# Seven-product chunks of the MLP up projection: pairs of chunks in quarters of 512 columns, in place of single chunks in quarters of 256

## The chip, the cores and the metric

The kernel runs on one core of a Trainium2 chip. The metric is the device time of one execution in microseconds (us). The numbers of the profile come from one profiled execution of the same program. The engines are named as the profile names them: PE (matmul), DVE (elementwise on vectors), ACT (activations and copies), POOL, and SP, which here only issues DMAs.

## The reference

A trunk of two layers on 256 tokens with a model width of 2048, in 32-bit floats. Each layer is a token mixer (forgetting attention in the first, dilated windows in the second) and an MLP with a hidden width of 8192:

```python
def sq_relu_mlp(h, w_up, w_down):
    a = jax.nn.relu(h @ w_up)
    return (a * a) @ w_down

def reference(x, ...):
    for i in range(DEPTH):                       # 2 layers
        h = rms_norm(x, mix_norm_g[i])
        mix = fox_attention(...) if i % 2 == 0 else dilated_attention(...)
        x = x + mix
        h = rms_norm(x, mlp_norm_g[i])
        x = x + sq_relu_mlp(h, mlp_w_up[i], mlp_w_down[i])
    return x
```

The change is in the MLPs alone.

## The kernel before

**Products.** The 256 tokens are two halves of 128. Weights are read in tiles of 256 rows x 512 columns (512 KB, a *raw* tile). Each is split into a high part `wh` (ACT casts) and a low part `wl` (DVE subtracts), and the activations are split alike, so one product of 32-bit numbers is three matmuls: high x high, high x low, low x high. A *plain step* uses one raw tile: 2 blocks of 128 rows x 2 token halves x 3 = 12 matmuls of 512 columns (`product_steps`). A plain product of one 512-column chunk takes 8 steps and gathers in one pair of PSUM banks, one bank for each token half.

**The MLP's order.** It goes in four blocks `b` of 2048 hidden columns. Each block has four up chunks `n` of 512 columns and then a down projection with four products. Relu and square follow each up chunk, and the result is turned (transposed) by DVE in blocks of 32 and by way of DRAM (`turn_up`), then split into `aTh` and `aTl`, which are the stationary operands of the down product.

**Seven products.** Ten of the sixteen up chunks of a layer (three in block 1, three in block 2, four in block 3) are computed by a scheme that needs seven block products where eight are usual. For each tile of 256 rows it sees four quarters of the weights (128 rows x 256 columns) and four of the activations (128 rows x 128 tokens). `token_sums` makes four sums of the activations' quarters once for each MLP; `sum_quarters` makes three sums of the weights' quarters for every raw tile on DVE (tile `quarters`). Such a *slice* takes two split tiles, first the quarters themselves (768 columns) and then the sums (1024 columns), and 7 x 3 = 21 matmuls of 256 columns into halves of four banks (`slice_steps`, table `SEVEN`). `halves_chain` recombines the seven sums. Slices are woven between the plain steps of the block before, at steps that are written out in the tables `BETWEEN`.

**Order and lookahead.** The program is written out by one recording order. Helper chains are generators that advance by one *tick*: one for every half of a plain step and for every part of a slice. Weights are split five tiles ahead of their use: `split` is called when a tile is used up and prepares the fifth after it. Raw tiles lie in a ring of five (`RAW_BUFS`); `next_load` asks for the next raw tile when the oldest has been split. All these loads, and the DMAs of `turn_up`, are issued by SP in that order, and each engine works through its instructions in that order.

**Banks.** `sums` takes banks from a pool of four, so two plain products in a row use different pairs. The slices use the other four banks. In blocks 0 to 2 the down products are evicted by `add_chain` (`late`): ACT scales two halves of each bank into tiles `y`, and POOL adds them to the residual by DMA. The down products of a block are grouped, two at a time (three in block 3), so that the first half of the hidden chunks is used first.

Of the kernel before, what the change touches and what calls it, by code (L numbers as in the profile page):

```python
# [17 lines left out]
P = 128  # L18
D = 2048
# [22 lines left out]
DOWN_PARTS = ((0, 8), (8, 16))  # L42
# [7 lines left out]
BETWEEN = (-6, -5, -4, -2, 0, 1, 2, 3, 7, 8, 9, 10, 11, 12, 13, 15, 18, 19, 21, 22, 23, 24, 25, 26)  # L50
FIRST_BETWEEN = (0, 1, 2, 3, 4, 5, 6, 8, 11, 12, 13, 14, 15, 16, 17, 18, 22, 23, 25, 26, 27, 28, 29, 30)


LAST_BETWEEN = (-10, -9, -8, -6, -5, -4, -3, -1, 3, 4, 5, 6, 7, 8, 9, 11, 14, 15, 16, 17, 18, 19, 20, 22, 25, 27, 28, 30, 31, 32, 33, 35)
# [51 lines left out]
def trunk(ctx: ExitStack, tc, x, fox_w_in, fox_b_f, fox_q_gain, fox_k_gain, fox_w_out, dil_w_in,  # L106
# [4 lines left out]

    def clear(steps):

        return steps + (jobs.now + steps + 1) % 2
# [24 lines left out]
    ps_acc = ctx.enter_context(tc.tile_pool(name="ps_acc", bufs=4, space=PSUM))  # L139
# [13 lines left out]
    spare = ps_acc.tile([P, NC], F32, tag="acc", name="spare")  # L153
# [101 lines left out]

    def add(w, rows, cols):

        for r in range(rows[0], rows[1], RAW_SUB * P):
            units.append((len(plan), "rows"))
            plan.append((w, r, cols))  # L260
            for at in woven["due"].get(woven["count"], ()):
                units.extend(((len(plan), "quarters"), (len(plan), "sums")))
                plan.append(at)
            woven["count"] += 1

# [16 lines left out]
    def in_halves():  # L282

        for b in range(1, 4):
            for i, at in enumerate((FIRST_BETWEEN, BETWEEN, LAST_BETWEEN)[b - 1]):
                yield 40 * b - 8 + at, b, i // 8, i % 8

    def add_mlp(l):
        woven["count"] = 0
        for at, b, n, pr in in_halves():  # L290
            woven["due"].setdefault(at, []).append((mlp_w_up[l], pr * RAW_SUB * P, [(b * D + n * NC, NC)]))
        for b in range(4):
            if b == 0:
                add_group(*((mlp_w_up[l], [(n * NC, NC)]) for n in range(2)))
            for n in ((2, 3), (3,), (3,), ())[b]:
                add(mlp_w_up[l], (0, D), [(b * D + n * NC, NC)])
            down = mlp_w_down[l][b * D:(b + 1) * D]
            together = 3 if b == 3 else 2
            add_group(*((down, [(n * NC, NC)]) for n in range(together)), parts=LAST_DOWN_PARTS if b == 3 else DOWN_PARTS)
# [27 lines left out]
    state = {"raw": 0, "split": 0}  # L327
    raws, splits = [], []

    def load():  # L330
# [3 lines left out]
        w, r, cols = plan[i]  # L334
        t = wpool.tile([P, RAW_SUB, NC], F32, tag="raw", name=f"raw{i}", bufs=RAW_BUFS)
        at = 0
        for c, width in cols:
            src = w[r:r + RAW_SUB * P, c:c + width].rearrange("(c p) n -> p c n", p=P)
            hold(t)
            for rows in [slice(k, k + 1) for k in range(RAW_SUB)] if i == 1 else [slice(0, RAW_SUB)]:  # L340
                nc.sync.dma_start(t[:, rows, at:at + width], src[:, rows])
            at += width
# [16 lines left out]
    def split_part(i, part):  # L359
        nonlocal summing  # L360
        n, of = units[i]
        raw, (hi, lo) = raws[n], splits[i]
        if of == "sums":
            raw = quarters.pop()
        if of == "quarters":
            flat_hi, flat_lo, flat = (x.rearrange("p k n -> p (k n)")[:, 0:3 * HC] for x in (hi, lo, raw))
            nc.scalar.copy(flat_hi, flat)  # L367
            for _ in summing or sum_quarters(n):
                pass
            summing = None  # L370
            nc.vector.tensor_sub(flat_lo, flat, flat_hi.bitcast(F32))  # L371
            return
        nc.scalar.copy(hi[:, part, :], raw[:, part, :])  # L373

        coming = i + 1 < len(units) and units[i + 1][1] == "quarters"
        if coming:
            summing = sum_quarters(units[i + 1][0])
            next(summing)
# [859 lines left out]
```

## Time and profile before

| | |
|---|---|
| time, median of 3 runs | 2097.87 us (2097.11 to 2098.36) |
| profiled execution | 2098.41 us |
| its span, first to last instruction | 2096.7 us |
| PE busy | 2089.2 us, 11515 matmuls |
| DVE busy | 1774.4 us |
| ACT busy | 1296.4 us |
| DMA | 518.28 MB, mean 247 GB/s |

In rows of groups stand line, engine, operation, output<-inputs, shape, count, then busy time in us and the mean of one in ns, then the idle time of the engine ahead of them and what ended it. In rows of the order of time stand start and duration in us. In rows of waits stand the total in us, how often, and the longest. In tables of stretches stand busy us and count of each engine, the granted PE clock, the DMA share and GB/s. In rows of DMA issues stands last the median time from issue to landing in us. `halves_n` are the banks of the slices, `acc` those of plain products, `hT_n` the split activations, `sums_n` their sums, `room_n` the work tile of `token_sums`.

### The profile page before, as it was taken

The page shows a single profiled execution, that of the slowest core. Times are in us where ns is not written, and L with a number is a line of the kernel's source. Part 1 is how long each engine was busy: PE and PEld are TensorE (multiplying, and loading weights), DVE is VectorE, ACT ScalarE, POOL GpSimd, SP SyncE. Part 2 cuts the span into 40 slices and gives each one's busy share as a digit, 9 for nine tenths or more (in the row PEclk, how much of TensorE's full clock was granted, in tenths as well). Part 3 has the DMA queues.
Part 4 walks back from the last instruction along what each step waited for, and adds up shares of the span by engine and source line. Part 5 has one row for each costly group of instructions (what it writes and reads, how often), then busy time and mean ns, then how long its engine had stood idle before and what let it go on. Part 6 is the DMA issues. An engine that isn't in the chain of part 4 may idle for free.

```text
span 2096.7 us, 32543 instructions
## 1 busy us (share of the span) xinstructions
PE 2089.2 (100%) x11515; PEld 1877.3 (90%) x11515; DVE 1774.4 (85%) x2613; ACT 1296.4 (62%) x1895; POOL 134.8 (6%) x142
## 2 busy tenths in 40 slices
PE   9999999999999999999999999999999999999999
PEld 7888888889999999998888888888899998999998
DVE  6888876889999999998768787767899989999974
ACT  6665654766666666664655665645666766666663
POOL 2000000000100100110010010000001101000100
PEclk9999999999999999999999999999999999999999
DMA  8888877887887977887877776867878878788884
GB/s 257 255 261 267 253 245 223 273 263 240 259 243 245 265 239 256 261 256 232 281 239 230 247 241 212 264 207 238 282 235 259 243 250 243 234 251 258 265 265 151
DMA packets 375010, 518.28 MB, mean 247 GB/s; under 512 B 43112, under 2 KB 176576, under 8 KB 374848
## 3 DMA queue, kind: packets, MB, share of 16 engines
q1 hardware_dynamic: 360608, 503.23, 75.7%
q0 software_dynamic: 13824, 12.59, 4.0%
q8 instruction: 90, 1.47, 0.3%
q14 instruction: 72, 0.59, 0.1%
q10 hardware_dynamic: 416, 0.39, 0.1%
HBM read 463.12 MB, written 40.39 MB: 240 GB/s over the span
## 4 chain that ended last, share of the span: by engine, by line
PE 95%; DVE 2%; DMA 1%; issue 1%; ACT 0%; SPq 0%; ACTq 0%; DVEq 0%
PE acc L434 25%; PE acc L435 25%; PE acc L436 25%; PE halves_n L1069 6%; PE halves_n L1068 6%; PE halves_n L1067 6%; DVE wl L379 1%; DMA raw<-in_mlp_w_up_dram 1%; ACT wh L373 0%; PE sc_d L746 0%; DMA x<-in_x_dram 0%; PE sc_f L746 0%; PE po_d L695 0%; PE sc_d L743 0%; PE acc L482 0%
## 5 line engine op out<-in xcount | busy, mean ns | idle before, releaser
L379 DVE TENSOR_TENSOR wl<-raw,wh 128x1024 fp32r<-128x1024 f32 (+1 forms) x643 | 774.8, 1212 | 228.4 <-ACT wh L373 223.8
L373 ACT CAST wh<-raw 128x1024 fp32r<-128x1024 f32 (+1 forms) x643 | 663.8, 1043 | 393.7 <-PE acc L436 302.0
L434 PE MATMUL acc<-wh,hT_n 128*128 128x512 f32 x1280 | 486.4, 380 | 0.3 <-ACT hT_n L577 0.3
L435 PE MATMUL acc<-wl,hT_n 128*128 128x512 f32 x1280 | 485.4, 379 | 0.0
L436 PE MATMUL acc<-wh,hT_n 128*128 128x512 f32 x1280 | 485.3, 379 | 0.0
L373 ACT CAST wh<-quarters 128x1024 fp32r<-128x1024 f32 x160 | 167.9, 1049 | 265.9 <-DVE quarters L397 239.8
L436 PEld LDWEIGHTS acc<-wh,hT_n 128*128 128x128 f32 x1280 | 241.9, 189 | 34.6 <-DVE hT_n L578 0.4
L434 PEld LDWEIGHTS acc<-wh,hT_n 128*128 128x128 f32 x1280 | 242.2, 189 | 32.8 <-ACT hT_n L577 0.6
L435 PEld LDWEIGHTS acc<-wl,hT_n 128*128 128x128 f32 x1280 | 242.2, 189 | 32.6 <-DVE wl L379 0.5
L379 DVE TENSOR_TENSOR wl<-quarters,wh 128x1024 fp32r<-128x1024 f32 x160 | 194.9, 1218 | 40.9 <-ACT wh L373 40.9
L434 PE MATMUL acc<-wh,aTh_n1a 128*128 128x512 f32 x512 | 194.3, 379 | 0.0
L435 PE MATMUL acc<-wl,aTh_n1a 128*128 128x512 f32 x512 | 194.2, 379 | 0.0
L436 PE MATMUL acc<-wh,aTl_n1a 128*128 128x512 f32 x512 | 194.1, 379 | 0.0
L435 PE MATMUL acc<-wl,aTh_n3a 128*128 128x512 f32 x480 | 182.4, 380 | 0.0
L434 PE MATMUL acc<-wh,aTh_n3a 128*128 128x512 f32 x480 | 182.1, 379 | 0.0
L436 PE MATMUL acc<-wh,aTl_n3a 128*128 128x512 f32 x480 | 181.9, 379 | 0.0
L1067 PE MATMUL halves_n<-wh,sums_n 128*128 128x256 f32 x640 | 176.2, 275 | 0.0
L1069 PE MATMUL halves_n<-wh,sums_n 128*128 128x256 f32 x640 | 176.0, 275 | 0.0
L1068 PE MATMUL halves_n<-wl,sums_n 128*128 128x256 f32 x640 | 176.0, 275 | 0.0
L371 DVE TENSOR_TENSOR wl<-raw,wh 128x768 fp32r<-128x768 f32 x160 | 152.0, 950 | 0.0
L367 ACT CAST wh<-raw 128x768 fp32r<-128x768 f32 x160 | 133.1, 832 | 26.5 <-PE acc L436 12.0
L942 POOL DMA_DIRECT2D x<-y_n x96 | 84.2, 1357 | 970.3 <-ACT y_n L941 837.1
(655 smaller groups left out, 3527.3 us busy)
## 6 DMA issues: line engine op xcount, KB each, us to landing
raw<-in_mlp_w_up_dram SPq DMA_DIRECT2D x256, 512.0 KB, 5.1
raw<-in_mlp_w_down_dram SPq DMA_DIRECT2D x256, 512.0 KB, 4.8
raw<-in_dil_w_in_dram SPq DMA_DIRECT2D x192, 256.0 KB, 3.7
raw<-in_fox_w_in_dram SPq DMA_DIRECT2D x94, 512.0 KB, 4.8
raw<-in_fox_w_out_dram SPq DMA_DIRECT2D x32, 512.0 KB, 4.7
raw<-in_dil_w_in_dram SPq DMA_DIRECT2D x32, 512.0 KB, 4.9
raw<-in_dil_w_out_dram SPq DMA_DIRECT2D x32, 512.0 KB, 4.2
x<-y_n POOLq DMA_DIRECT2D x96, 128.0 KB, 5.9
```

What stands on the lines that cost most here:

```text
L367: nc.scalar.copy(flat_hi, flat)
L371: nc.vector.tensor_sub(flat_lo, flat, flat_hi.bitcast(F32))
L373: nc.scalar.copy(hi[:, part, :], raw[:, part, :])
L379: nc.vector.tensor_sub(lo[:, part, :], raw[:, part, :], hi[:, part, :].bitcast(F32))
L434: nc.tensor.matmul(acc[t], ah[:, tok], hi, start=first, stop=False)
L435: nc.tensor.matmul(acc[t], ah[:, tok], lo, start=False, stop=False)
L436: nc.tensor.matmul(acc[t], al[:, tok], hi, start=False, stop=last)
L942: nc.gpsimd.dma_start(xt[n][:, t, h * HC:h * HC + HC], y, accum_op=ALU.add)
L1067: nc.tensor.matmul(to, ah, hi, start=pr == 0 and not half, stop=False, skip_group_check=True)
L1068: nc.tensor.matmul(to, ah, lo, start=False, stop=False, skip_group_check=True)
L1069: nc.tensor.matmul(to, al, hi, start=False, stop=pr == KC // 2 - 1, skip_group_check=True)
```

## The change

The seven-product scheme now works on two neighbouring chunks, `n` and `n + 1`, at once. The quarters of the weights are 128 rows x 512 columns, one column half from each chunk, and each matmul has 512 columns. The number of chunks by seven products stays ten a layer: five pairs (`WIDE`). The other six chunks are plain (`UP_ALONE`).

Six of the seven products of a row block are done in three *slots* of two products, 6 matmuls each. A row block of a pair brings two raw tiles, each by two DMAs. The slots use three split tiles in turn: the quarters that lie crosswise (`crossed`), differences, and sums. DVE makes the differences from both raw tiles, and the sums out of them, in the tile `quarters`. The raw tiles are used up only when the sums are made. The seventh product (first quarter of the weights with first quarter of the activations) is done after all eight row blocks, in a *sweep*: four raw tiles hold the needed rows of the first chunk, read a second time, and their four slots add into bank 0 after ACT has copied the first product out of it.

The table of places is replaced by a rule (`wide_slots`): from step 17 of each MLP on, one slot follows each plain step, and two after the last step of each plain product; a pair's sweep and the next pair are set apart by at least one plain step.

The six sums of a pair take six whole banks: the four of before and one pair from the pool of plain products. So while pairs are under way every plain product of the MLP uses the same pair of banks (`turn["only"]`), and the evictions are recorded inside the product's last step and no longer after it. The down products of blocks 0 to 2 are no longer grouped. In `turn_up` the way through DRAM is held open until the place for the result is free, and the tiles are read back only then.

```diff
-DOWN_PARTS = ((0, 8), (8, 16))
-SEVEN = ((0, 0, 2, 5), (1, 0, 0, 4), (2, 0, 1, 0), (3, 0, 7, 6), (0, 1, 5, 3), (1, 1, 6, 2), (2, 1, 4, 1))
+PRODUCTS = (((0, 1, 5), (1, 0, 0)), ((2, 0, 1), (3, 1, 3)), ((4, 0, 2), (5, 1, 6)))
+WIDE = ((1, 0), (2, 0), (2, 2), (3, 0), (3, 2))
+WIDE_FROM = 17
+UP_ALONE = ((2, 3), (2, 3), (), ())
+def wide_slots():
+    todo = []
+    for b, n in WIDE:
+        todo += [(b, n, what, pr) for pr in range(KC // 2) for what in range(3)] + [None]
+        todo += [(b, n, 3, pr) for pr in range(0, KC // 2, 2)] + [None]
+    count = WIDE_FROM
+    while todo:
+        room = full = 2 if count % 8 == 7 else 1
...
-    ps_acc = ctx.enter_context(tc.tile_pool(name="ps_acc", bufs=4, space=PSUM))
+    ps_acc = ctx.enter_context(tc.tile_pool(name="ps_acc", bufs=2, space=PSUM))
...
+    def add_slot(w, c, what, pr):
...
+        if what == 0:
+            woven["at"] = len(plan)
+            for columns in ((NC, 0), (0, NC)):
+                plan.append([((k, slice(0, NC)), w[r + k * P:r + k * P + P, c + columns[k]:c + columns[k] + NC])
+                             for k in range(RAW_SUB)])
+        units.append((woven["at"], ("crossed", "differences", "sums")[what]))
...
+        if of == "crossed":
+            sums_of[0] = work.tile([P, RAW_SUB, NC], F32, tag="sd", name=f"quarters{n}", bufs=1)
+            nc.vector.tensor_sub(sums_of[0], raw, raws[n + 1][:, 1, :].unsqueeze(1).to_broadcast([P, RAW_SUB, NC]))
+        elif of != "rows":
+            raw = sums_of[0]
         nc.scalar.copy(hi[:, part, :], raw[:, part, :])
         nc.vector.tensor_sub(lo[:, part, :], raw[:, part, :], hi[:, part, :].bitcast(F32))
+        if of == "differences":
+            nc.vector.tensor_add(raw[:, 0, :], raws[n][:, 0, :], raw[:, 1, :])
+            nc.vector.tensor_sub(raw[:, 1, :], raws[n + 1][:, 0, :], raw[:, 0, :])
...
-        n = units[state["split"] - 1][0]
-        whole = state["split"] == len(units) or units[state["split"]][0] != n
-        if whole and state["raw"] == n + RAW_BUFS:
+        n, of = units[state["split"] - 1]
+        spent.update({"rows": (n,), "differences": (n, n + 1)}.get(of, ()))
+        while state["done"] in spent:
+            state["done"] += 1
+        while state["raw"] < min(len(plan), state["done"] + RAW_BUFS):
             load()
...
-    def sums(pool=ps_acc, tag="acc"):
+    def sums(pool=ps_acc, tag=None):
+        if tag is None:
+            tag = f"acc{turn['next'] if turn['only'] is None else turn['only']}"
+            turn["next"] = 1 - turn["next"]
...
+            if post is not None and k == KC - 1:
+                jobs.spawn(post(acc))
...
-                if t == 0:
-                    yield clear(1)
...
-    def slice_steps(tag, banks, pr):
+    def slot_steps(tag, banks, what, pr):
+        hi, lo = splits[used[0]]
+        for bank, i, a, of in [(0, i, 4, pr + i) for i in range(2)] if what == 3 else [(*x, pr) for x in PRODUCTS[what]]:
...
+            nc.tensor.matmul(banks[bank], ah, wh, start=what < 3 and of == 0, stop=False, **alone)
+            nc.tensor.matmul(banks[bank], ah, wl, start=False, stop=False, **alone)
+            nc.tensor.matmul(banks[bank], al, wh, start=False, stop=of == KC // 2 - 1, **alone)
...
-                     scale=tag, group=3 if b == 3 else 2, parts=LAST_DOWN_PARTS if b == 3 else DOWN_PARTS, **(after if b == 3 else {"late": True}))
+                     scale=tag, group=3 if b == 3 else 0, parts=LAST_DOWN_PARTS, **(after if b == 3 else {"late": True}))
```

How the work stands in a row on three engines follows, first before and then now. On DVE before, one slice and the plain step ahead of it in the down projection of block 1; `raw220` is the plain tile, `raw221` the slice's:

```order
L391 TENSOR_TENSOR quarters221_6244<-raw221_6130 128x512
L379 TENSOR_TENSOR wl245_6242<-raw220_6112,wh245_6241 128x1024
L395 TENSOR_TENSOR quarters221_6244<-raw221_6130,quarters221_6244 128x256
L397 TENSOR_TENSOR quarters221_6244<-raw221_6130,quarters221_6244 128x256
L371 TENSOR_TENSOR wl246_6267<-raw221_6130,wh246_6266 128x768
```

On DVE now, a row block of the first pair, with `raw174` and `raw175` its two tiles, and plain tiles and a turning between (down projection of block 0):

```order
L395 TENSOR_TENSOR quarters174_4843<-raw174_4745,raw175_4780 128x1024
L399 TENSOR_TENSOR wl180_4842<-raw174_4745,wh180_4841 128x1024
L399 TENSOR_TENSOR wl181_4855<-raw176_4783,wh181_4854 128x1024
L1015 STREAM_TRANSPOSE turned_n1a0_3_0_4858<-a_n1a0_3_0_4825 128x4x4x32
L399 TENSOR_TENSOR wl182_4881<-quarters174_4843,wh182_4880 128x1024
L401 TENSOR_TENSOR quarters174_4843<-raw174_4745,quarters174_4843 128x512
L402 TENSOR_TENSOR quarters174_4843<-raw175_4780,quarters174_4843 128x512
```

One difference of full size and the sums stand where three short sums stood, and both raw tiles are read until the last row. On SP before, the loads of the slices (up) and plain steps (down) alternate one by one:

```order
L341 DMA raw240_6697<-in_mlp_w_up_dram 128x2x512
L341 DMA raw241_6712<-in_mlp_w_down_dram 128x2x512
L341 DMA raw242_6730<-in_mlp_w_up_dram 128x2x512
L341 DMA raw243_6748<-in_mlp_w_down_dram 128x2x512
L341 DMA raw244_6766<-in_mlp_w_up_dram 128x2x512
```

On SP now, at the same row block of the first pair and the next (`x2` are the two DMAs of one raw tile):

```order
L373 DMA raw178_4833<-in_mlp_w_down_dram 128x2x512
L354 DMA held_n1a0_3_0_4859<-turned_n1a0_3_0_4858 32x4x128 x4
L373 DMA raw179_4886<-in_mlp_w_up_dram 128x512 x2
L373 DMA raw180_4889<-in_mlp_w_up_dram 128x512 x2
L373 DMA raw181_4892<-in_mlp_w_down_dram 128x2x512
L354 DMA held_n1a0_3_1_4895<-turned_n1a0_3_1_4894 32x4x128 x4
L373 DMA raw182_4911<-in_mlp_w_down_dram 128x2x512
```

Both tiles of the next row block (`raw179`, `raw180`) are recorded together, behind the sums of `raw174` and `raw175`. On PE before, the end of one plain product (a slice stands last) and the start of the next, in banks of its own:

```order
L1069 MATMUL halves_n1_1_2_0_5733<-wh219_5717,sums_n1_1_1_4002 128x256
L434 MATMUL acc220_0_5832<-wh220_5744,aTh_n1a0_0_4355 128x512
L435 MATMUL acc220_0_5832<-wl220_5745,aTh_n1a0_0_4355 128x512
L436 MATMUL acc220_0_5832<-wh220_5744,aTl_n1a0_0_4356 128x512
L434 MATMUL acc220_1_5833<-wh220_5744,aTh_n1a0_0_4355 128x512
```

On PE now, the end of the plain product `acc194`, one of the two slots' products, and the start of `acc211`, in the same two banks:

```order
L449 MATMUL acc194_0_5169<-wh208_5369,aTl_n1a0_3_5016 128x512
L447 MATMUL acc194_1_5170<-wh208_5369,aTh_n1a0_3_5015 128x512
L448 MATMUL acc194_1_5170<-wl208_5370,aTh_n1a0_3_5015 128x512
L449 MATMUL acc194_1_5170<-wh208_5369,aTl_n1a0_3_5016 128x512
L1090 MATMUL wide_n1_2_0_acc00_5277<-wh209_5387,sums_n1_1_0_4001 128x512
...
L1092 MATMUL wide_n1_2_0_tp1_5274<-wh210_5397,sums_n1_2_1_4112 128x512
L447 MATMUL acc211_0_5491<-wh211_5415,aTh_n1a0_0_4395 128x512
```

Between the last matmul into `acc194_0` and the first into `acc211_0` stand three matmuls of the other bank and two slots of six.

More of the change, by code (lines that the diff above doesn't have):

```diff
@@ L1062, in slice_steps @@
             if a < 4:
[L1063 removed]
+                ah, al = (x[:, a, :] for x in sumT[tag, of])
             else:
[L1065 to L1068 removed]
```

226 lines of the change are left out of this document (109 added, 117 removed).

## The prediction

> **What bounds the kernel now.** I read the page's busy time and its chain first, then the waits of PE.
>
> ```profile
> PE 2089.2 (100%) x11515; PEld 1877.3 (90%) x11515; DVE 1774.4 (85%) x2613; ACT 1296.4 (62%) x1895; POOL 134.8 (6%) x142
> PE 95%; DVE 2%; DMA 1%; issue 1%; ACT 0%; SPq 0%; ACTq 0%; DVEq 0%
> PE halves_n L1067 <- DVE c_n3a L1042: 1.3, 1, 1.3
> ```
>
> PE is busy in 2089.2 of the 2096.7 us, and 95% of the chain that ended last is matmuls. PE's largest wait inside the program is 1.3 us. So time is saved by taking work from PE, and lost by any wait that is put in front of it.
>
> How near the other engines stand is read from the stretches in which slices of seven products are woven between plain products (MLP of the first layer, 450 to 950 us).
>
> ```profile
> core 0: us, PE busy (x) PEld busy (x) DVE busy (x) ACT busy (x) POOL busy (x), PEclk, DMA share, GB/s
> 450.00:550.00 100.00, 100.00 (x637) 92.56 (x636) 94.94 (x136) 65.64 (x90) 7.24 (x8) 1.00 0.78 239
> ...
> sum 500.00, PE 500.00 PEld 461.04 DVE 469.85 ACT 329.99 POOL 42.94; mean PE 100.00 PEld 92.21 DVE 93.97 ACT 66.00 POOL 8.59
> ```
>
> PE never pauses there, at clock 1.00, but DVE is busy 469.85 of 500 us: 94%. The lookahead of five split tiles just hides DVE. It is the engine that would be next.
>
> **The PE work, which is the gain.** The time of a matmul is read from starts, since the durations overlap.
>
> ```profile
> 900.18 0.27 PE L1067 MATMUL halves_n<-wh,hT_n 128*128 128x256 f32 x1
> ...
> 902.52 0.38 PE L434 MATMUL acc<-wh,aTh_n1a 128*128 128x512 f32 x1
> ...
> 905.11 0.27 PE L1067 MATMUL halves_n<-wh,hT_n 128*128 128x256 f32 x1
> ```
>
> From 900.18 to 902.52 lie the 21 matmuls of one slice: 111.4 ns each. From 902.52 to 905.11 lie the 12 matmuls of a plain step: 215.8 ns each. Each layer has ten chunks by seven products before and five pairs of chunks after, so 20 chunks x 8 x 21 = 3360 matmuls of 256 columns become 1680 of 512. Plain matmuls keep their number. 3360 x 111.4 = 374.3 us goes, 1680 x 215.8 = 362.5 us comes: **-11.8 us**, all on the path. It is 7.0 ns for each pair of short matmuls.
>
> [...]
>
> **DVE and ACT.** The operations that go and come, by their rows:
>
> ```profile
> L379 DVE TENSOR_TENSOR wl<-raw,wh 128x1024 fp32r<-128x1024 f32 x637 | 770.7, 1217 | 226.8 <-ACT wh L373 222.1 <-DMA blocks_n1a<-turned_n1a 1.4 <-DMA blocks_n3a<-turned_n3a 1.4
> L371 DVE TENSOR_TENSOR wl<-raw,wh 128x768 fp32r<-128x768 f32 x160 | 152.0, 950 | 0.0
> L391 DVE TENSOR_TENSOR quarters<-raw 128x512 f32<-128x512 f32 x160 | 109.3, 683 | 5.6 <-DMA raw<-in_mlp_w_up_dram 3.2
> L397 DVE TENSOR_TENSOR quarters<-raw,quarters 128x256 f32<-128x256 f32 x160 | 67.6, 422 | 4.8
> L395 DVE TENSOR_TENSOR quarters<-raw,quarters 128x256 f32<-128x256 f32 x160 | 66.7, 417 | 0.0
> L1024 DVE TENSOR_TENSOR aTl_n1a<-turned_n1a,aTh_n1a 128x512 fp32r<-128x512 f32 x32 | 21.9, 683 | 0.0
> L1002 DVE STREAM_TRANSPOSE turned_n1a<-c_n1a 128x256 f32<-128x256 f32 x40 | 15.2, 418 | 0.0
> L1002 DVE STREAM_TRANSPOSE turned_n1a<-a_n1a 128x512 f32<-128x512 f32 x12 | 8.4, 703 | 0.0
> L949 DVE TENSOR_TENSOR x<-x,acc 128x512 f32<-128x512 f32 x16 | 10.2, 678 | 0.0
> L1038 DVE TENSOR_TENSOR c_n1a<-halves_n,c_n1a 128x256 f32<-128x256 f32 x10 | 4.2, 424 | 0.3
> ```
>
> Two chunks before: 16 slices x (0.95 + 0.68 + 0.42 + 0.42 + 1.22 = 3.69) = 59.0 us, and for each chunk seven recombinations at 0.42, four transposes at 0.42 and two splits at 0.68, 6.0 us: 71.0 us. A pair after: for each of 8 row blocks one difference 128x1024 (not in the trace; as long as the 128x1024 subtraction, 1.22), three splits at 1.22 and two of 128x512 at 0.68, 6.24 us; four sweep splits, 4.9; six recombinations at 0.68, four transposes at 0.70, four splits at 0.68, 9.6: 64.4 us. Ten pairs spare DVE 66 us. ACT casts 128x1024 seven times for every two row blocks instead of 128x1024 and 128x768 four times each; it is at 66% and gains too. Off the path: 0, but it widens the 6% that DVE has left.
>
> The **start of each MLP** is the exception: the first pair begins at step 17 and no longer at step 32, beside the token sums and the first chunks' turning.
>
> ```profile
> L546 DVE TENSOR_TENSOR room_n<-hT_n 128x512 f32<-128x512 f32 x16 | 10.8, 674 | 0.0
> L551 DVE TENSOR_TENSOR room_n<-room_n 128x256 f32<-128x256 f32 x16 | 6.8, 426 | 0.5
> L550 DVE TENSOR_TENSOR room_n<-room_n 128x128 f32<-128x128 f32 x16 | 4.7, 292 | 0.5
> L557 DVE TENSOR_TENSOR sums_n<-room_n,sums_n 128x512 fp32r<-128x512 f32 x16 | 10.9, 684 | 0.0
> 695.13 0.41 DVE L1041 TENSOR_TENSOR c_n1a<-c_n1a,halves_n 128x256 f32<-128x256 f32 x1
> 695.46 0.41 DVE L1042 TENSOR_TENSOR c_n1a<-c_n1a,halves_n 128x256 f32<-128x256 f32 x1
> ```
>
> Steps 17 to 38 hold 22 plain splits (26.8), 8 row blocks (49.9), about five token sums of 0.67 + 2 x 0.29 + 0.43 + 0.68 = 2.37 (11.8) and four chunks' turning of 2 x 0.70 + 2 x 0.68 (11.1): 99.6 us of DVE durations against 22 x 2.59 + 144 x 0.2158 = 88.1 us of PE. Queued operations start 0.08 us before the one ahead ends (0.41 long, 0.33 apart); over some 111 operations that is 9, which leaves about 3 us too much. The lookahead of five tiles (about 9 us of PE) takes it if it is full. Ends: 0, and 5 us a layer if half the lookahead is gone. I take 1.5 a layer, **+3 us**, nearer the low end, since the following steps have slack.
>
> **Loads.** Here is the new wait that I fear most. A row block of a pair needs two raw tiles at once, and both stay in use until the last of the sums; a plain tile stands between them in the ring of five, so the next block's two tiles are asked for only when DVE has finished the sums of this one.
>
> ```profile
> raw<-in_mlp_w_up_dram SPq DMA_DIRECT2D x256, 512.0 KB, 5.1
> raw<-in_dil_w_in_dram SPq DMA_DIRECT2D x192, 256.0 KB, 3.7
> DMA to landing us min/median/max: 3.6/4.9/9.3
> ```
>
> (The last row is for all raw tiles from 450 to 950 us.) This makes a loop: landing, difference 1.22, split 1.22, plain split 1.22, split 1.22, two sums 1.37, landing again. DVE's part is 6.2 us. Three row blocks fill eight steps and nine slots: 8 x 2.59 + 54 x 0.2158 = 32.4 us of PE, 11.66, 11.66 and 9.07 (where two slots stand together). With 5.1 us a loop is 11.3 us. In the short one, one or no plain split lies inside and only one of the two tiles is late; with 3.7 plus 0.4 for the second issue it is 9.1 to 10.3 us. Three loops: 31.7 to 32.9 against 32.4. So it is about even on the median landing, and the five tiles ahead absorb a spread of a few us in each pair. Ends: 0 with 4.9 us, and 80 x 0.5 = 40 us with half a us more on every landing (the rows reach 9.3). I take **+1 us**, by the median row. What also grows is hidden: 21 MB of second reads for the sweeps (4% of 518 MB) and 200 more issues on SP, which is at 0% of the chain; they count through the landing time.
>
> **One pair of banks.** A plain product now starts in the banks that the product before it has just left. On ACT the evictions are queued behind the cast of the tile four ahead.
>
> ```profile
> 674.01 1.54 ACT L941 ACTIVATE y_n<-acc,rstd_n 128x256 f32<-128x256 f32 x4
> ACT wh L373 <- DVE quarters L397: 239.8, 122, 3.7
> ```
>
> From the last matmul into bank 0 to the next product stand three matmuls and two slots, 15 x 0.2158 = 3.2 us; two of the four evictions take 0.8. The margin is about 2.4 us. ACT's waits for DVE are 2.0 us in the mean (239.8/122) and at most 3.7. So a mean wait costs nothing and the longest 1.3; 32 product ends give 0 to 42 us. I take **+1.5 us**, by the mean: 0.5 for each of the two ends of a third block (steps 143 to 144), where no slot covers the eviction, and 0.5 for the rest. The copy of bank 0 ahead of a sweep and its relu ahead of the next pair are each covered by a plain step of 2.59 us. The wait for recombined banks (1.3 us, above) can go: -1.3. The turning through memory is issued at the same distance in steps and is needed by the first products later than it takes; 0.
>
> **Sum.** The profiled execution took 2098.41 us: the span of 2096.7 and 1.7 around it, 0.5 over the median 2097.87. 2098.4 - 11.8 + 3 + 1 + 1.5 - 1.3 = 2090.8, less 0.5 to stand beside the median: **2090.3 us**, 0.36% faster.
>
> **Rivals.**
> - *The loop of raw tiles sets the pace* (slower). For it: 80 loops that are even at the median, and landings up to 9.3 us. Against it: DVE is spared 66 us. It decides from a mean landing of about 5.3 us. At 5.6 us it is 80 x 0.5 = 40 us too long, of which sweeps and lookahead take perhaps 2 us a pair: +20 instead of +1, **2109 us**.
> - *The bank waits eat the gain* (no change). If DVE still holds ACT as now, a quarter of a us at each of 32 ends and 1.5 us more at each MLP start are 8 + 3 us on top of the sum, less the 1.5 that I had for the banks: **2100 us**.
> - *The short matmuls are not dearer by themselves*: the 3.5 ns a matmul over half of 215.8 would belong to the slice, its change of operands, and the slots would pay it too; two thirds of the gain go, **2098 us**. Against it: all 21 starts of the slice are evenly spaced. [...]
> - *A chunk comes late to a down product*, as the down products are no longer grouped for three of four blocks. The steps from a chunk's end to its use fall from ten to six. Six down blocks (three a layer) start so; each 2 us late is 12 us: **2102 us**, at the border of slower. Against it: the turning is issued as many steps ahead as before, counted in slots.
>
> **Chances.** Forecast 0.45; raw loop 0.26; bank waits 0.18; dear slots 0.03; late chunks 0.08, counted as slower. Within 0.2% (4.2 us, about what a measurement of this kernel can tell from no change) lie the second and third rival: 0.21. Slower: 0.34. Faster: 0.45. The forecast's own range is 2083 (no wait at all) to 2093.6. For 8 in 10 the range goes from 2082 to 2114, which leaves out the worse part of the raw loop.
>
> **What would show it.** Starts 215.8 ns apart in the slots; PE at 100% in the MLPs with DVE below 94%; waits of PE of up to 3 us in all in the first 130 us of each MLP, if any. If the raw loop rules, the row blocks' differences on DVE wait for raw from memory, often and for about 1 us, and PE for wl. If the banks rule, PE's first matmul of a product waits for y_n on ACT. I am wrong if DVE's idle time grows while PE waits.

## The result: 3.5% slower

| | before | after |
|---|---|---|
| time, median | 2098.1 us (2097.11 to 2098.36) | 2171.5 us (2166.17 to 2176.72) |
| ratio | | 1.0351, 95% interval 1.0325 to 1.0376 |
| span of the profiled execution | 2096.7 us | 2164.1 us |

The forecast was 2090.3 us, and its range ended at 2114. The page of the changed kernel, busy time and chain of work:

```profile
PE 2100.8 (97%) x9835; PEld 1825.7 (84%) x9835; DVE 1746.7 (81%) x2213; ACT 1285.8 (59%) x1775; POOL 138.2 (6%) x142
...
PE 39%; DMA 9%; DVE 8%; ACT 2%; issue 2%; SPq 1%; ACTq 0%; DVEq 0%
```

The chain is no longer PE's alone (its shares add up to 61% of the span; the profile does not tell the rest). The sum over the stretch from 450 to 950 us of the same trace:

```profile
sum 500.00, PE 477.58 PEld 411.69 DVE 431.08 ACT 305.97 POOL 38.88; mean PE 95.52 PEld 82.34 DVE 86.22 ACT 61.19 POOL 7.78
```

PE pauses there for 22 us where it never had, and DVE, down from 469.85 to 431.08 us, idles as well. The waits of the whole execution (L447 to L449 are the three matmuls of a plain step, L958 the eviction of a down product, L1090 the first matmul of a slot, L1052 the copy of a pair's first product out of its bank, L998 the relu of a plain chunk, L398 the cast to `wh`, L395 the differences, L402 the second sum):

```profile
PE acc L447 <- ACT y_n L958: 15.4, 9, 3.3
PE acc L449 <- DVE aTl_n1a L1039: 10.6, 8, 2.4
...
PE wide_n_tp L1090 <- ACT c_n3a L1052: 4.4, 2, 3.7
...
PE acc L447 <- ACT a_n3a L998: 3.9, 3, 2.9
...
ACT wh L398 <- DMA raw<-in_mlp_w_down_dram: 138.5, 60, 5.0
...
ACT wh L398 <- DMA raw<-in_mlp_w_up_dram: 57.2, 44, 3.6
DVE quarters L395 <- DMA raw<-in_mlp_w_up_dram: 51.0, 29, 4.7
```

ACT and DVE wait 246.7 us for raw tiles (138.5 + 57.2 + 51.0), more than half of it not at the differences but at the casts of the plain tiles between them (`mlp_w_down`). PE stands still for 63.3 us (2164.1 less 2100.8): 15.4 are waits for evictions of down products, 20.4 for other work of ACT on the banks (all rows of `c_n` and `a_n`), 14.5 for `aTl` of both MLPs. How that reaches PE is seen in order of time, here near 540 us:

```profile
538.14 0.69 DVE L402 TENSOR_TENSOR quarters<-raw,quarters 128x512 f32<-128x512 f32 x1
538.16 0.87 SPq L373 DMA_DIRECT2D raw<-in_mlp_w_up_dram  x2
539.13 1.40 SPq L373 DMA_DIRECT2D raw<-in_mlp_w_down_dram  x3
539.88 1.05 ACT L398 CAST wh<-raw 128x1024 fp32r<-128x1024 f32 x1
...
545.94 1.04 ACT L398 CAST wh<-raw 128x1024 fp32r<-128x1024 f32 x1 [5.01 <-PE wide_n_tp L1092]
546.89 1.04 ACT L398 CAST wh<-quarters 128x1024 fp32r<-128x1024 f32 x1
547.84 1.56 ACT L958 ACTIVATE y_n<-acc,rstd_n 128x256 f32<-128x256 f32 x4
...
548.72 0.48 PE L447 MATMUL acc<-wh,aTh_n1a 128*128 128x512 f32 x1 [2.89 <-ACT y_n L958]
...
550.14 0.69 DVE L402 TENSOR_TENSOR quarters<-raw,quarters 128x512 f32<-128x512 f32 x1
```

One row block of a pair needs two raw tiles, and three plain tiles stand beside it: five, the whole ring. The ring moves on in order, so plain tiles that were split long ago stay behind the two that the sums still need. When the sums are made, SP asks for everything in one burst: the last up tile of the next row block and three plain tiles. Of its five DMAs the last four, one of 256 KB and three of 512 KB, took:

```profile
DMA to landing us min/median/max: 3.2/7.1/8.3
```

The first plain tile of the burst, issued at 539.13, took 6.7 us to land, which is at 545.8, and its cast starts at 545.94. (The row names PE, whose matmul ended in the same tenth of a us.) The last matmul into the finished down product's banks started at 542.86, but its four evictions, queued behind this cast and the next, started at 547.84, and PE, which must write into that one pair of banks, waits 2.89 us. From one second sum to the next are 12.00 us (538.14 to 550.14), in which PE started only 40 matmuls, 8.6 us of work at 0.2157 us each; a row block with its plain steps needs an estimated 11.66 (54 of them).

On SP eight DMAs of a turning stood ahead of the burst, until 538.1, and the first DMA of the burst started at 538.16:

```profile
529.93 8.13 SPq L354 DMA_DIRECT2D held_n1a<-turned_n1a  x8
```

The difference at 541.86 then waited 0.63 us for the up tile. How much of all the waits is due to this order on SP stays open; no run takes the turnings off its queue.

### The profile page after: what moved, and what is told of

It is laid out like the page before. It is cut to its first block, busy times and chain, and to the rows that moved or that the text cites. A ratio compares the mean times of both kernels' runs of the same rounds, so it can differ in the third digit from the quotient of the medians.

```text
span 2164.1 us, 29143 instructions
## 1 busy us (share of the span) xinstructions
PE 2100.8 (97%) x9835; PEld 1825.7 (84%) x9835; DVE 1746.7 (81%) x2213; ACT 1285.8 (59%) x1775; POOL 138.2 (6%) x142
## 4 chain that ended last, share of the span: by engine, by line
PE 39%; DMA 9%; DVE 8%; ACT 2%; issue 2%; SPq 1%; ACTq 0%; DVEq 0%
PE acc L449 11%; PE acc L447 11%; PE acc L448 11%; DMA raw<-in_mlp_w_down_dram 6%; DVE wl L399 5%; DMA raw<-in_mlp_w_up_dram 3%; ACT wh L398 2%; DVE quarters L401 1%; SPq L373 1%; DVE quarters L395 1%; SPq L354 0%; DVE turned_n3a L1015 0%; DVE aTl_n3a L1039 0%; PE wide_n_tp L1090 0%; PE wide_n_acc L1091 0%
## 5 line engine op out<-in xcount | busy, mean ns | idle before, releaser
L399 DVE TENSOR_TENSOR wl<-raw,wh 128x1024 fp32r<-128x1024 f32 (+1 forms) x763 | 922.5, 1214 | 298.1 <-ACT wh L398 291.5
L398 ACT CAST wh<-raw 128x1024 fp32r<-128x1024 f32 (+1 forms) x763 | 790.4, 1044 | 586.7 <-PE acc L449 307.4
L447 PE MATMUL acc<-wh,hT_n 128*128 128x512 f32 x1280 | 489.7, 383 | 7.3 <-ACT a_n3a L998 3.1
L449 PE MATMUL acc<-wh,hT_n 128*128 128x512 f32 x1280 | 487.6, 381 | 0.0
L447 PEld LDWEIGHTS acc<-wh,hT_n 128*128 128x128 f32 x1280 | 243.6, 190 | 42.7 <-ACT a_n3a L998 3.9
L449 PEld LDWEIGHTS acc<-wh,hT_n 128*128 128x128 f32 x1280 | 243.4, 190 | 34.5 <-DVE hT_n L595 0.4
L398 ACT CAST wh<-quarters 128x1024 fp32r<-128x1024 f32 x160 | 167.3, 1045 | 174.9 <-DVE quarters L402 124.0
L447 PE MATMUL acc<-wh,aTh_n1a 128*128 128x512 f32 x512 | 196.5, 384 | 11.0 <-ACT y_n L958 9.9
L449 PE MATMUL acc<-wh,aTl_n1a 128*128 128x512 f32 x512 | 196.2, 383 | 10.6 <-DVE aTl_n1a L1039 10.6
L447 PE MATMUL acc<-wh,aTh_n3a 128*128 128x512 f32 x480 | 184.0, 383 | 4.4 <-ACT y_n L958 3.6
L449 PE MATMUL acc<-wh,aTl_n3a 128*128 128x512 f32 x480 | 183.6, 383 | 3.9 <-DVE aTl_n3a L1039 3.9
L395 DVE TENSOR_TENSOR quarters<-raw,raw 128x1024 f32<-128x1024 f32 x80 | 97.5, 1219 | 52.2 <-DMA raw<-in_mlp_w_up_dram 51.0
L447 PEld LDWEIGHTS acc<-wh,aTh_n1a 128*128 128x128 f32 x512 | 97.5, 191 | 28.1 <-ACT y_n L958 13.2
L449 PEld LDWEIGHTS acc<-wh,aTl_n1a 128*128 128x128 f32 x512 | 97.5, 191 | 27.5 <-DVE aTl_n1a L1039 14.1
L448 PEld LDWEIGHTS acc<-wl,aTh_n1a 128*128 128x128 f32 x512 | 97.6, 191 | 14.5 <-DVE wl L399 1.1
L447 PEld LDWEIGHTS acc<-wh,aTh_n3a 128*128 128x128 f32 x480 | 91.6, 191 | 19.5 <-ACT y_n L958 5.6
```

The source lines that it names most:

```text
L395: nc.vector.tensor_sub(sums_of[0], raw, raws[n + 1][:, 1, :].unsqueeze(1).to_broadcast([P, RAW_SUB, NC]))
L399: nc.vector.tensor_sub(lo[:, part, :], raw[:, part, :], hi[:, part, :].bitcast(F32))
L447: nc.tensor.matmul(acc[t], ah[:, tok], hi, start=first, stop=False)
L448: nc.tensor.matmul(acc[t], ah[:, tok], lo, start=False, stop=False)
L449: nc.tensor.matmul(acc[t], al[:, tok], hi, start=False, stop=last)
```

## The experiments

Runs are named by the numbers of these paragraphs. Theory **A**: the two raw tiles are held too long for a ring of five; casts wait for loads, and evictions and PE stand behind the casts. **B**: the one pair of banks is the cause, whenever loads arrive. **C**: the added 21 MB and 200 issues load DMA and SP.

**1. The raw tiles given back early.** The sums are made of the differences alone, leaving the raw quarters out, and both raw tiles are released after the first split.

```diff
-nc.vector.tensor_add(raw[:, 0, :], raws[n][:, 0, :], raw[:, 1, :])
+nc.vector.tensor_add(raw[:, 0, :], raw[:, 0, :], raw[:, 1, :])
-spent.update({"rows": (n,), "differences": (n, n + 1)}.get(of, ()))
+spent.update({"rows": (n,), "crossed": (n, n + 1)}.get(of, ()))
```

> The sums of a row block are made from the differences alone and both raw tiles count as used up after the first of its three split tiles; the number, size and place of all loads, DVE operations, casts, matmuls and evictions stay (the up results are wrong, since the sums leave the raw quarters out). Theory A (the two raw tiles are held too long in the ring of five, so casts on ACT wait for loads, and evictions and PE behind them): nearly all of the loss goes, 2088 to 2105 us, and the casts' waits for raw tiles (138.5 + 57.2 us) fall below 60. Theory B (the waits come from the single pair of banks): under 15 us of gain, 2155 to 2171. Theory C (DMA traffic and the doubled number of issues): no gain, 2165 to 2175.

2120.5 us, ratio 1.0109 (1.0093 to 1.0124): 51 us of the 73 go, with the same loads and the same banks. B and C fall as main cause. ACT's waits for raw tiles of the MLPs in this run, under the 60 us that A allowed:

```profile
ACT wh L398 <- DMA raw<-in_mlp_w_down_dram: 21.7, 18, 2.5
ACT wh L398 <- DMA raw<-in_mlp_w_up_dram: 10.7, 11, 1.6
```

A missed its upper bound by 15 us, so it is not the whole.

**2. No evictions.** The late down products are neither evicted nor added.

```diff
-nc.scalar.activation(y, by_column(acc[t])[:, 0, h, :], AF.Copy, ...)
-nc.gpsimd.dma_start(xt[n][:, t, h * HC:h * HC + HC], y, accum_op=ALU.add)
+pass
```

> The down products of blocks 0 to 2 are not evicted and not added to the residual (left out of the result): no wait for their banks is left. Theory A: the direct waits for y (15 us) and part of the half-clock stretches go, but the lag of the casts stays and shows at the other places: 2135 to 2158 us. Theory B: most of the loss goes, 2095 to 2120 us. Theory C: 2150 to 2165.

2144.8 us, ratio 1.0225 (1.0208 to 1.0242), inside A's range. ACT still waits 117.5 us for `mlp_w_down`. The evictions carry at most some 27 us of the delay to PE (the edit also takes their work off ACT and POOL's DMAs off the queues); they don't start it.

**3. A ring of four**, `RAW_BUFS = 4`.

> The ring of raw tiles has four buffers and not five, nothing else. Theory A: the loop is then shorter of a tile in every row block, and the loss grows steeply, by 80 to 250 us, to 2250 to 2420 us. Theory B: 2171 to 2200 us. Theory C: 2171 to 2190.

2290.6 us, ratio 1.0919 (1.0898 to 1.094): one tile less costs 119 us, as A has it.

**4. A ring of seven.** Room for two raw tiles comes from one split tile less ahead.

```diff
-RAW_BUFS = 5
-W_BUFS = 5
+RAW_BUFS = 7
+W_BUFS = 4
```

> Split tiles are made four and not five ahead, and the memory so freed gives the ring seven raw tiles. Theory A: the loads come in time, the shorter lookahead costs a little, 2090 to 2120 us. Theory B: evictions stand behind fewer casts, some gain, 2140 to 2170 us. Theory C: more traffic ahead changes nothing and the shorter lookahead costs: 2170 to 2200.

2116.6 us, ratio 1.009 (1.0075 to 1.0105). This is inside A's range. Of ACT's waits for raw tiles in the MLPs one row is left:

```profile
ACT wh L398 <- DMA raw<-in_mlp_w_down_dram: 3.9, 2, 2.1
...
raw<-in_mlp_w_up_dram SPq DMA_DIRECT2D x320, 256.0 KB, 5.7
```

The pieces of the pairs land later than in the changed kernel (5.7 against 3.9 us), and it does no harm: with two tiles more in the ring they are asked for sooner.

**5. Its control: four split tiles, ring of five.**

> The changed kernel with four split tiles ahead in place of five, and its ring of five raw tiles kept: the control for the run with four split tiles and seven raw ones (2116.6 us), so that the two differ in the ring alone. Raw tiles held too long (A): the ring is still five, so nothing is won, and one split tile less ahead costs a little: 2171 to 2195 us, ACT's waits for raw from memory together above 170 us. If the gain of that run came from the shorter lookahead and not from the ring (for example from ACT's casts standing less far ahead of the evictions): 2115 to 2130 us, with ACT's waits for raw still long.

2157.9 us, ratio 1.0297 (1.027 to 1.0325). The ring alone is thus worth 41 us here (2157.9 to 2116.6). The shorter lookahead, which I had expected to cost time, won 13.5 us by the medians, though the intervals of the two ratios touch (1.0325); A's range for this run began at 2171, and ACT's waits for raw tiles of the MLPs were 146.3 us (97.8 + 48.5) where A had named 170. Up to an estimated 6.5 us of the 13.5 belong to PE's clock, whose mean over the profiled span was 0.994 in the changed kernel (0.006 x 2164 = 13.0 us lost) and 0.997 here (0.003 x 2156 = 6.5). PE's wait for evictions fell from 15.4 to 7.7 us; that fits one cast less standing ahead of them on ACT, but no run shows this by itself.

```profile
PE acc L447 <- ACT y_n L958: 7.7, 4, 3.0
```

**6. Sums made right after the differences**, into a tile of their own, four split tiles, ring of six.

> All of the result is computed here, in a different order: the two sums of a row block are made right after its differences, into a tile of their own, and both raw tiles are given back there, one cast earlier than before; four split tiles ahead, ring of six. A: the loop loses about 2.6 us of plain split, cast and wait, and the ring has one tile more: 2105 to 2125 us, ACT's waits for raw below 40 us in all. If what held things up was the order of DVE's queue (the sums, 1.4 us, now stand in front of the split that PE needs first): 2125 to 2150 us with PE waiting for wl.

2124.0 us, ratio 1.0123 (1.0107 to 1.0138), inside A's range. The run changes the ring and the time of release together, so it does not part the two.

**7. The start of each MLP.** On run 4's kernel the first pair takes its split tiles from the raw quarters; its differences and sums are left out, and its raw tiles are given back after the third split.

```diff
+if n in plain:
+    raw = raws[n + 1] if of == "differences" else raw
-if of == "crossed":
+elif of == "crossed":
```

> On the kernel with four split tiles and seven raw ones (2116.6 us). The first pair of each MLP gets its split tiles from the raw quarters themselves: its difference and its two sums on DVE (2.6 us for each of eight row blocks) are left out, so those two chunks are wrong. If the start of each MLP is bound by DVE (S): PE's excess of about 12 us in the first 30 us of the two MLPs goes to under 3, total 2103 to 2109 us, with no wait of PE for wl there. If it is bound by loads or by the token sums' own latency: 2113 to 2118 us, and PE goes on waiting there for wl or sums.

2106.9 us, ratio 1.0042 (1.0027 to 1.0057). The first row is 427 to 453 us in run 4, the second the same stretch here:

```profile
427.00:453.00 26.00, 23.89 (x106) 19.23 (x105) 25.66 (x34) 15.68 (x20) 0.00 (x0) 1.00 0.69 232
```

```profile
427.00:453.00 26.00, 26.00 (x123) 22.75 (x122) 25.57 (x34) 18.98 (x25) 0.00 (x0) 1.00 0.83 276
```

DVE is full in both (25.66 and 25.57 of 26 us); with less to do for each slot PE gets through without a pause. Leaving this work of DVE out wins 9.7 us in the two MLPs together (2116.6 less 2106.9), inside the range; that is what their starts cost here.

**8. The ends of the down blocks**, on run 4's kernel: the fourth block begins in the other pair of banks, and a turned chunk is cast three ticks after its read-back is asked for, and not six.

```diff
-turn.update(next=turn["only"], only=None)
+turn.update(next=1 - turn["only"], only=None)
-yield clear(6)
+yield clear(3)
```

> On the kernel with four split tiles and seven raw ones (2116.6 us), two edits that show in different waits. The fourth block's first product takes the other pair of banks: PE's wait for the eviction at step 144 (2.6 us in the first MLP, 1.6 in the second) goes if the one pair of banks is its cause. The cast of a turned chunk is queued three steps after its read-back is asked for in place of six: if the late chunk (PE waiting for aTl at the starts of down products, 5.7 us, and the half clock behind it) comes from the number of steps, it goes. Both: 2104 to 2110 us. If the data itself is back late from memory, ACT and DVE wait for it in the queue and PE waits as before: 2111 to 2120 us.

2147.6 us, ratio 1.0237 (1.0222 to 1.0252): 31 us slower than run 4, and in neither range. The wait at step 144 is gone, but ACT now waits for the turned tiles:

```profile
ACT aTh_n3a L1037 <- DMA back_n3a<-held_n3a: 42.7, 22, 3.6
ACT aTh_n1a L1037 <- DMA back_n1a<-held_n1a: 42.4, 21, 3.4
...
PE acc L448 <- DVE wl L399: 20.9, 27, 1.6
```

It is A's mechanism with another transfer: an instruction that was queued too early on ACT waits for memory, and whatever stands behind it is late. Runs 9 and 10 keep the edit of the banks without this loss, so the 31 us belong to the sooner cast.

**9. Token sums on GpSimd**, with the other pair of banks, on run 4's kernel.

```diff
-nc.vector.tensor_add(to.rearrange("p (i t) n -> p i (t n)", i=2), ...)
+nc.gpsimd.tensor_add(to.rearrange("p (i t) n -> p i (t n)", i=2), ...)
...
-nc.vector.tensor_add(a21, a21, a22)
+nc.gpsimd.tensor_add(a21, a21, a22)
```

> All of the result is computed. On the kernel with four split tiles and seven raw ones (2116.6 us): the fourth block's first product takes the other pair of banks, and the four additions of each row block's token sums go from DVE to GpSimd (1.69 us of DVE for each of 16 row blocks; five of them fall into the crowded first 30 us of each MLP, 8.4 us). If the start of each MLP is bound by DVE, about two thirds of the 12 us lost there come back and PE's wait at step 144 (2.6 and 1.6 us) goes: 2102 to 2109 us. If GpSimd holds DVE up as much as it spares it, or the sums come late from it: 2112 to 2125 us, with PE waiting for sums.

2122.0 us, ratio 1.0121 (1.0106 to 1.0136), slower than run 4 and in the second range. Rows of DVE and POOL near 1536 us:

```profile
1535.53 0.68 DVE L1039 TENSOR_TENSOR aTl_n3a<-back_n3a,aTh_n3a 128x512 fp32r<-128x512 f32 x1
1536.13 2.30 DVE L399 TENSOR_TENSOR wl<-raw,wh 128x1024 fp32r<-128x1024 f32 x1
```

```profile
1535.76 1.60 POOL L563 TENSOR_TENSOR room_n<-hT_n 128x512 f32<-128x512 f32 x1 [4.44 <-ACT aTh_n3a L1037]
1537.44 1.32 POOL L566 TENSOR_TENSOR room_n<-room_n 128x128 f32<-128x128 f32 x1
```

DVE's subtraction takes 2.30 us beside POOL's additions; another of the same shape, at 1533.79, when POOL was idle, took 1.22. Why it takes longer there is not shown.

**10. Tightened casts**, with the other pair of banks, on run 4's kernel: DVE's subtraction for a turned chunk is queued in the same tick as ACT's cast.

```diff
 nc.scalar.copy(ah, src)
-yield 1
 nc.vector.tensor_sub(al, src, ah.bitcast(F32))
```

> All of the result is computed. On the kernel with four split tiles and seven raw ones (2116.6 us): the other pair of banks for the fourth block, and the two halves of a turned chunk are cast and subtracted without the step that lay between cast and subtraction, so that the second half is ready two steps sooner while its first cast stays where it was. If the late chunk is a matter of the steps between its two halves: PE's waits for aTl (5.7 us) go below 2, the half clock behind them goes: 2105 to 2110 us. If they stand behind other work on DVE: 2110 to 2115 us, with the waits for aTl as before.

2112.1 us, ratio 1.0075 (1.0058 to 1.0092). PE's waits for `aTl` (5.7 us in run 4) are gone from the list, but a wait of 2.2 us for `wl` near 931 us has come up, so the time missed its range by 2 us and fell into the other one, whose reason (waits for `aTl` as before) does not hold. With the edits of 9 and 10 together:

> All of the result is computed. The three edits together on the kernel with four split tiles and seven raw ones. If each cost is its own: 2116.6 less 3 (banks), 8 (start), 6 (late chunks): 2095 to 2104 us, at or a little below the kernel before. If they share one cause, so that one hides the other: 2104 to 2112 us.

2119.3 us, ratio 1.0108 (1.0093 to 1.0123): neither range. Beside run 10 GpSimd costs 7 us.

**11. The first pair from step 22**, on the kernel of 10.

```diff
-WIDE_FROM = 17
+WIDE_FROM = 22
-room = full = 2 if count % 8 == 7 else 1
+room = full = 2 if count % 8 == 7 or count % 8 == 3 and 80 <= count < 144 else 1
```

> All of the result is computed. On the kernel with the other pair of banks and the tightened casts (2112.1 us): the first pair of each MLP starts at step 22 in place of 17, and two slots stand together twice in eight steps from step 80 on, so that the last pair ends at step 143 as before. If the 11 us lost in the first 30 us of the two MLPs come from DVE's token sums and turnings meeting the first row blocks, the later start spreads them: under 5 us left there, 2104 to 2109 us. If the sums of DVE's work up to step 46 set it wherever the pair starts, or the denser slots lose it again behind step 80 (PE waiting for wl there): 2110 to 2120 us.

2098.56 us against 2098.64, ratio 0.9997 (0.9988 to 1.0007): level with the kernel before, the best of all, and below both ranges. But not for the reason that I gave:

```profile
427.00:453.00 26.00, 23.60 (x109) 20.03 (x108) 25.55 (x36) 15.83 (x20) 0.00 (x0) 1.00 0.74 234
...
850.00:950.00 100.00, 100.00 (x465) 87.55 (x465) 86.81 (x92) 64.03 (x77) 11.13 (x14) 1.00 0.90 279
```

The start still pauses for 2.4 us with DVE full. What went are pauses behind 800 us, where the later slots now stand at other places. In run 10 the second stretch was:

```profile
850.00:950.00 100.00, 97.76 (x446) 84.87 (x445) 81.58 (x85) 61.37 (x74) 11.10 (x14) 0.98 0.86 268
```

**12. Other places.** From step 24:

> All of the result is computed. On the kernel that starts the first pair at step 22 (2098.6 us): it starts at step 24, and two slots stand together twice in eight steps from step 80 on, so that the last pair still ends at step 143. About 9 us are still lost in the first 30 us of the two MLPs. If they hang on where the first row blocks meet the token sums and the turning of the first chunks, two steps later takes 2 to 5 us more off them: 2093 to 2097 us. If they hang on the amount of DVE's work alone, they stay: 2097 to 2101 us.

2110.9 us, ratio 1.0065 (1.005 to 1.008). No slot lies behind step 23 any more, and PE waits there for the eviction of a plain chunk, once in each MLP:

```profile
PE acc L447 <- ACT a_n3a L998: 1.6, 1, 1.6
...
PE acc L447 <- ACT a_n1a L998: 1.5, 1, 1.5
```

With the doubled slots from step 64 on it was 2109.0 us (1.0058, 1.0041 to 1.0075). From step 23, doubled from 88 on:

> All of the result is computed. Four split tiles, seven raw ones, the other pair of banks, tightened casts, the first pair of each MLP from step 23, two slots together twice in eight steps from step 88 on. With the start at step 24, PE waited 1.5 us for the eviction of the third plain chunk (no slot lay behind step 23), and 0.9 us at each of four product ends whose slots had moved off; with the start at 22 it waited for wl. If each of these is only a matter of which step a slot follows: both are covered at 23, 2091 to 2097 us, at or below the kernel before. If DVE's total up to step 47 sets the start: 2096 to 2101 us, as with 22.

2110.5 us, ratio 1.0058 (1.0044 to 1.0072): the eviction's wait falls to 0.7 us, others rise. With the start at 22 and the doubled slots from 104 on it was 2102.6 us (1.0022, 1.0012 to 1.0031), from 48 on 2118.9 us (1.0094, 1.0077 to 1.0111), with one wait of 6.1 us for `aTl`:

> All of the result is computed. As before, from step 48 on, so that the last pair ends at step 139, where four steps without slots lie in front of the last down block. If only the start is left: 2096 to 2100 us. If the waits follow where slots stand against product ends, moved sweeps open new ones, and the last down products before the fourth block have no slot behind them that covers an eviction: 2101 to 2115 us.

Of these five runs two came out as one of their theories had it: the second from step 24, within 2 us of the first, and the one doubled from 104 on. Against run 11 a start one or two steps later cost 10 to 12 us, and another place for the doubled slots alone 4 to 20. Which place costs what stays open but for the rows shown. None of these was faster than the kernel before.

**13. The ring put back.** The kernel from step 23 with five raw and five split tiles, as in the changed kernel.

> All of the result is computed. The same kernel with the ring of five raw tiles and five split tiles ahead put back, as in the changed kernel: the later start, the other pair of banks and the tightened casts stand without the longer ring. If the raw tiles held too long are the main cause (A), they cost their 45 to 55 us here too: 2135 to 2155 us, with ACT's waits for raw above 150 us in all. If the start and the ends were what really held the ring up (late evictions making DVE late, and DVE the raw tiles): 2100 to 2125 us.

2160.7 us, ratio 1.0298 (1.0284 to 1.0313):

```profile
ACT wh L398 <- DMA raw<-in_mlp_w_down_dram: 123.5, 57, 5.2
ACT wh L398 <- DMA raw<-in_mlp_w_up_dram: 53.6, 51, 2.5
DVE quarters L395 <- DMA raw<-in_mlp_w_up_dram: 49.5, 26, 4.3
```

Ring and lookahead together cost 50 us (2160.7 less 2110.5) on a kernel with other starts and ends too, where the changed kernel and run 4 are 54.9 us apart. The waits for raw tiles are as A has them (177.1 us at the casts); the time is 6 us above A's range, and far from the other theory's.

## Why the prediction was wrong

- **PE work, -11.8: right.** In the changed kernel the starts stand as forecast: from 535.31 (first row) to 545.45 (last) are 47 spacings of 0.2157 us, slots and plain steps alike; no run shows the two thirds of the gain that the rival on dear slots took off. Run 11, with that PE work and level in time, shows where the gain goes: PE is busy 8.1 us less than in the kernel before (2081.1 against 2089.2), and idle 9.6 us more (17.1 of 2098.2 us against 7.5 of 2096.7). Why the busy time does not show the whole 11.8 stays open.

```profile
535.31 0.38 PE L1090 MATMUL wide_n_tp<-wh,hT_n 128*128 128x512 f32 x1
...
545.45 0.38 PE L1092 MATMUL wide_n_tp<-wh,sums_n 128*128 128x512 f32 x1
```

The busy times of run 11:

```profile
PE 2081.1 (99%) x9835; PEld 1818.7 (87%) x9835; DVE 1744.6 (83%) x2213; ACT 1296.4 (62%) x1775; POOL 135.9 (6%) x144
```

- **Loads, +1 with ends 0 and 40: the step that failed.** It measured 41 us for the ring alone (run 5 to run 4); with the fifth split tile ahead it was 50 (run 13) and 54.9 (the changed kernel to run 4). The two tiles that its loop counted mostly come soon enough: 3.9 us for a piece, below the 5.3 from which the loop was to decide, and 51 of the 80 differences show no wait for them. The other 29 waited 51.0 us, so the loop is part of the loss. Later still are the plain tiles of the same burst, 5.8 us in the median, and the casts that wait for them (138.5 us).

```profile
raw<-in_mlp_w_down_dram SPq DMA_DIRECT2D x256, 512.0 KB, 5.8
raw<-in_mlp_w_up_dram SPq DMA_DIRECT2D x320, 256.0 KB, 3.9
```

So the step saw that the ring is held, and took the next pair's tiles for the only ones that are held back; the plain tiles behind them are too, since the ring moves on in order. And it did not ask who is queued behind a late plain tile: on ACT it is the evictions and the copies and relus that free the other banks. The rival on the raw loop named the ring, with the same loop, and priced it at 20 us. Taken in the order of the runs, the 81 us from the forecast to the result are 41 for the ring, 13.5 for the fifth split tile ahead, which the sum had as help and not as a cost, 18.0 for starts, ends and places (run 4 to run 11), and 8.3 that stay open (run 11 to the forecast).

- **DVE and ACT, 0: right in sign, and in the durations.** DVE was to be spared 66 us. Added up, the durations of its instructions in the two traces fell by 61.5 (1913.6 to 1852.1), but its busy time, in which overlaps count once, fell by 27.7 (1774.4 to 1746.7). It has 400 instructions fewer, and by the 0.08 us of overlap that the prediction used at the MLP's start, an estimated 400 x 0.08 = 32 us was time that overlapped anyway; the traces have 33.8. The room won on DVE is thus less than half of what the 66 us promised.
- **Start of each MLP, +3: too small.** 9.7 us (run 7), near the upper end of 5 a layer. The 3 us that were left over in the sum did not vanish in the lookahead; that is with four split tiles ahead, and no run measures it with five.
- **One pair of banks, +1.5: right in place, small in size.** The eviction at step 144, forecast at 0.5 for each layer, took 2.4 us in the first MLP of run 4. Edit 8 removed it. Most other waits of PE for these evictions came with late loads: in run 1, with the same banks, they fall from 15.4 to 3.9 us.

```profile
933.85 0.48 PE L447 MATMUL acc<-wh,aTh_n1a 128*128 128x512 f32 x1 [2.44 <-ACT y_n L958]
```

- **Turning through memory, 0: wrong.** 5.7 us of waits for `aTl` in run 4, half of the 12 us that the rival on late chunks named. Queueing the subtraction sooner took them away; queueing the cast sooner cost 31 us.
- **What would show it.** "I am wrong if DVE's idle time grows while PE waits": that is what the stretch from 450 to 950 us shows.

## What to carry to other kernels

Where a step holds several tiles of a ring that advances in order, count all tiles that lie between the first one it takes and its release: if they fill the ring, nothing is asked for ahead, and the loads come in bursts (four DMAs of one burst here took 3.2 to 8.3 us to land, 7.1 in the median). Then look on each engine for what is queued behind an instruction that waits for memory; that, and not the waiting instruction, may be what the busiest engine needs, as it was here: PE waited 2.89 us for evictions that stood on ACT behind a late cast. The saving of 0.6% in matmuls was smaller than what these waits cost.

## What the runs showed of the hardware

Two things. The granted clock of PE stood at half in short stretches of the changed kernel, near pauses of PE. PE waited 2.30 us ahead of a matmul at 955.66 us, and the 6 us from 957 to 963 ran at 0.50, with 11 matmuls started (and one more wait, of 1.48 us) where 6 us at 0.2157 us each have about 28:

```profile
940.00:950.00 10.00, 10.00 (x48) 8.76 (x48) 7.90 (x10) 7.51 (x11) 0.00 (x0) 1.00 0.86 293
950.00:956.00 6.00, 3.70 (x18) 2.93 (x17) 2.52 (x4) 3.75 (x8) 0.47 (x1) 1.00 0.83 290
957.00:963.00 6.00, 4.52 (x11) 3.33 (x11) 2.90 (x4) 2.73 (x5) 2.60 (x5) 0.50 0.99 220
```

The clock's records hold five such stretches of 3.41 or 6.83 us, 27.3 us together, so at most half of that, 13.7 us, was lost by them; the kernel before and run 11 have none inside. Each begins inside a pause of PE or up to 1.4 us behind one: 1.75, 2.30, 2.88, 1.96 and 3.45 us ahead of the matmuls at 441.49, 955.66, 1558.16, 1620.93 and 1971.65. The length of a pause alone does not decide: after the longest, 3.71 us ahead of a matmul at 1951.74, the clock stayed at 1.00, as it did after 3.33 us at 750.00. What sets the half clock off is not shown. The other is DVE beside GpSimd (run 9): a subtraction of 128x1024 took 2.30 us beside POOL's additions and 1.22 with POOL idle.
